# Cross attention's maxima ahead of a block's low split, its sums inside the second query projection, squares added on VectorE, and more halved products

## The chip, the cores and the metric

The kernel runs on one core of a Trainium2 chip. The metric is the device time of one execution in microseconds (us). The median of three runs of the kernel before is 655.46 us (655.09 to 655.58).

The names of the engines in the profile are: PE is TensorE (matmuls), PEld is the load of TensorE's stationary operand, DVE is VectorE, ACT is ScalarE, POOL is GpSimd, SP is SyncE, whose queue issues the loads of weights. PE, ACT, DVE and POOL each run their own queue in order and wait for each other by semaphores.

## The reference, cut to what matters

Two layers, 256 positions, width 1024, everything in f32. Each layer adds three parts to the hidden state `h`:

```
h = h + mixer(rmsnorm(h, norm_mix_g[layer]))
h = h + memory_cross_attention(rmsnorm(h, norm_xa_g[layer]), rmsnorm(mem, norm_mem_g[layer]), ...)
h = h + conv_ffn(rmsnorm(h, norm_ffn_g[layer]), ...)
```

- The mixer of layer 0 has 16 heads of width 64, eight of stick-breaking attention and eight of softmax attention with rotary queries and keys. That of layer 1 is 16 softmax heads with a forget gate. Both have a combined q/k/v projection (1024 x 3072) and an output projection (1024 x 1024).
- Cross attention has four heads of width 64: `q = h @ w_q` (1024 x 256), keys and values from `mem` (256 rows), a softmax over the 256 memory rows, and an output projection (256 x 1024).
- `conv_ffn` is a gated MLP: up (1024 x 5632), a causal depthwise convolution of width 3, silu times value, down (2816 x 1024).
- `rmsnorm(x, g) = x * rsqrt(mean(x*x) + 1e-6) * g`: it needs the sum of the squares of all 1024 channels of a row.

A last rmsnorm ends it.

## The kernel before, in words

**Layout and precision.** `h` is held transposed: eight tiles of 128 channels x 256 positions. A matrix product is done in three terms. Each operand is split into a high part (`fp32r`, an ACT copy) and a low part (DVE: the operand less its high part), and hi*hi, hi*lo and lo*hi are summed in PSUM; each is one PE instruction of 128x128 by 128x256. A projection onto 128 outputs over 1024 channels is thus 24 such products.

**Weights.** `block()` (L125) loads 128 x 1024 weights into `raw` through SP's queue, lets ACT write `whi` (L133) and DVE write `wlo` (L134), as a rule in two pieces of 512 columns, in the feed-forward part in one of 1024. Five pairs `whi`/`wlo` exist; a new block waits until PE has used the block five earlier.

**Order.** Only PE's order is written out by hand (L1046). The order of ACT, DVE and POOL is made by the framework's scheduler when the kernel is built, with the place of an instruction in the program as its priority. Two helpers bend it. `order()` puts one instruction behind another of the same engine. `fence(skip, on_act, on_dve)` (L122) makes the four blocks that follow after `skip` further blocks come behind the given instructions: their `whi` behind `on_act`, their `wlo` behind `on_dve`.

**Norms.** `rmsnorm`'s scale is applied late. `Normed.step()` writes the split of `h * g`: `xh` on ACT (L184), `xl` on DVE (L185). `Stats.add()` squares an `h` tile on ACT (L235) and adds it to the squares so far on POOL (L241). `Stats.sums()` (L261) sums over the partitions by four matmuls of one column (L266), DVE makes the mean (`ms`, L269) and POOL the power of -0.5 (`rcol`, L273). `spread()` (L277) turns that column into a row by two transposes on PE (L280) and an ACT copy. `residual()` (L566) adds a projection to `h[j]` on DVE (L567), then calls `Normed.step()` and `Stats.add()`.

**Mixer.** A `Pipe` counts projections with `tick()` and runs what is due at a count. `VISITS` says at which counts the attention of head pairs is done between projections (`visit()`, L611): outputs, scores, transposes or weights. In layer 0 `mem.spread` is due at count 16 by itself, between two projections (L632). At the end come eight blocks of the output projection: o0 to o3 (begun early), o4 to o6 in banks `sc`, o7 in a bank `acc`, each followed by its `residual`.

**Cross attention.** `cross()` (L797) projects q in two halves of 128 (channels 0 to 6 of both, then channel 7 of both), copies them out on DVE (`mq`, L806), and starts the value projection with a hook: after 13 of its 24 products come `st.sums()`, the score products of the four heads (L770), and the softmax: per head a maximum on DVE (`mx`, L778), a multiplication by `rcol` (L779), two exponentials on ACT (`xp`, L783), a reciprocal and two multiplications on DVE (L785, L787). Then come the second half of the value projection, transposes of the weights (L792), copies (`xpt`, L795), weights times values (L829), the split of the outputs (`gh`, `gl`), the output projection with its blocks `xa_o`, and eight residuals. The `fence` at L808 keeps the low splits of the `xa_o` blocks, and of the first two feed-forward blocks, behind the copy of the first `mq`.

**Feed-forward.** f counts 22 pairs of blocks. The pair f=0 is multiplied channel by channel, as `xh`, `xl` come in (L913). In f=1, `st.sums` is a hook after 6 products of the first block, `st.spread` one after 11 of the second.

**Halved products.** `product(..., halves)` (L286) does one product in two instructions of 128 columns with the same stationary operand. `HALVES` (L37) names the projections of the mixers in which one is halved, and the index of the product in it. In `proj_nat`, which makes v for positions 0 to 127 (t=0) and 128 to 255 (t=1), only t=0 can have one.

Of the kernel before, what the change touches and what calls it, by code (L numbers as in the profile page):

```python
# [17 lines left out]
P = 128  # L18
T = 256
# [16 lines left out]
           (26, (6, 7), (), ())))  # L36
HALVES = ({"q3": 8, "o3": 8}, {"k0": 18, "q1": 8, "k3": 8, "v2": 3, "q6": 8, "mk": 8, "o2": 8})  # L37
EPS = 1e-6
# [40 lines left out]
def trunk(ctx: ExitStack, tc: tile.TileContext, a: dict, out: bass.AP):  # L79
# [148 lines left out]
    class Stats:  # L228
# [4 lines left out]
        def add(self, t):  # L233
            sq = tmp.tile([P, T], F32, tag="sq", name="sq", bufs=3)
            nc.scalar.activation(sq, t, AF.Square)  # L235
            self.n += 1
            if self.n == KD and not self.one:
                self.parts = [self.acc, sq]
            else:
                if self.acc is not None:  # L240
                    nc.gpsimd.tensor_tensor(sq, sq, self.acc, op=ALU.add)  # L241
                self.acc = sq
                self.parts = [sq]
# [49 lines left out]

    def proj(b, off, xs, ps, first=True, last=True, m=P, hooks={}, skip=False, halve=None):
        n = 0
        for k, (xh, xl) in enumerate(xs):
            s = slice(off + k * m, off + k * m + m)
            end = last and k == len(xs) - 1
            for w, x in ((b.hi, xh), (b.hi, xl), (b.lo, xh)):
                product(ps[:m], w[:, s], x, n == halve, start=first and n == 0, stop=skip or end and w is b.lo,  # L300
                        skip_group_check=skip)
                n += 1
                if n in hooks:
                    hooks[n]()
        return ps
# [16 lines left out]

    def proj_nat(bs, xs, t, ps, hooks={}, halve=None):
        s = slice(t * P, (t + 1) * P)
        n = 0
        for k, (xh, xl) in enumerate(xs):
            b = bs[k // 4]
            w = slice((k % 4) * T, (k % 4 + 1) * T)
            for x, y in ((xh, b.hi), (xh, b.lo), (xl, b.hi)):
                product(ps, x[:, s], y[:, w], n == halve, start=n == 0, stop=n == 3 * KD - 1)  # L330
                n += 1
                if n in hooks:
                    hooks[n]()
# [258 lines left out]
    def mixer(layer, st, xs):  # L592
# [3 lines left out]
        pipe = Pipe()  # L596
        halves = HALVES[layer].get
        outs = [None] * 8
# [12 lines left out]
        def visit(out, prod, weigh):  # L611
# [12 lines left out]
            if layer == 0 and pipe.now == 8:  # L624
                rope_tables(st)
            for n in prod:
                for hd in heads[n]:
                    hd.scores()

        if layer == 0:  # L630
            pipe.at(13, mem.sums)
            pipe.at(16, lambda: mem.spread(bank(psO, "po")))  # L632
            pipe.at(6, lambda: rope_sines(heads[1][1].last))
# [3 lines left out]
        for g in range(4):  # L637
# [78 lines left out]
            def values():  # L716
                b = [block(w[6 * g + 2]), block(w[6 * g + 3])]
                for t in range(2):
                    ps = proj_nat(b, xs, t, (accA if g else accS)(),
                                  halve=None if t else halves(f"v{g}"))  # L720
                    v.append(evac_col(ps, st, t, "v", 6))
# [29 lines left out]
        for i in range(j, KD):  # L751
            residual(i, proj(block(w_out[i]), 0, outs, (accS, accS, accS, accA)[i - j]()), nst, nxt)
        return nst, nxt.res, ms, ks

    def mem_keys(layer, ms, pipe):
        ks = []
        for i in range(2):
            ps = proj(block(a["xa_k"][layer, i]), 0, ms, accA(), halve=None if i else HALVES[layer].get("mk"))
            ks.append(evac_row(ps, mem, "mk", False))
# [3 lines left out]
    class Cross:  # L763
# [10 lines left out]
        def scores(self):  # L774
            s = self.s
            mx = tiny.tile([P, 2], F32, tag="mx", name="mx", bufs=6)
            sm = tiny.tile([P, 2], F32, tag="sm", name="sm", bufs=6)
            nc.vector.tensor_reduce(mx, s.rearrange("p (t m) -> p t m", t=2), AX.X, ALU.max, negate=True)  # L778
            nc.vector.tensor_mul(mx, mx, self.st.col)  # L779
# [6 lines left out]
            for t, c in enumerate(cut):  # L786
                nc.vector.tensor_scalar(p[:, c], p[:, c], sm[:, t:t + 1], None, op0=ALU.mult)  # L787

        def weigh(self, copy):
# [7 lines left out]
    def cross(layer, st, xs, ms, ks):  # L797

        hd = []
        bq = [block(a["xa_q"][layer, i]) for i in range(2)]  # L800
        acc = [proj(bq[i], 0, xs[:7], accS(), last=False) for i in range(2)]
        for i in range(2):
            proj(bq[i], 7 * P, xs[7:], acc[i], first=False)
        for i in range(2):
            q = parts.tile([P, T], F32, tag="part", name="mq", bufs=NP)
            evac = nc.vector.tensor_scalar(q, acc[i], SCALE, None, op0=ALU.mult)  # L806
            if i == 0:
                fence(2, None, evac)  # L808
            hd += [Cross(j, q, ks[i], st) for j in range(2)]

        def scores():
            st.sums()
            both_products(hd[:2])
            both_products(hd[2:])
            for x in hd:
                x.scores()

        b = [block(a["xa_v"][layer, i]) for i in range(2)]
        v = [evac_col(proj_nat(b, ms, 0, bank(psO, "po", T), hooks={13: scores}), mem, 0, "mv", 2)]
        v.append(evac_col(proj_nat(b, ms, 1, accA()), mem, 1, "mv", 2))  # L820
        copied = [x.weigh(nc.vector.tensor_copy if i % 2 else nc.scalar.copy) for i, x in enumerate(hd)]
# [35 lines left out]
    def ffn(layer, st, xs):  # L857
# [58 lines left out]
        for f in range(KF):  # L916
# [3 lines left out]
            for i in range(2):  # L920
# [11 lines left out]
                else:  # L932
                    acc = (accS, accA)[i if full else n % 7 % 2]()
                    n += 1
                pss.append(proj(w, 0, xs if f < RAW else xn, acc, first=not (pair and i), hooks=hooks,
                                skip=pair, halve=20 if f == 1 and i == 1 else None))
            if f == 0:
# [201 lines left out]
```

## Time and profile before

| what | us |
|---|---|
| median of three runs (lowest, highest) | 655.46 (655.09, 655.58) |
| the profiled execution, its own time | 655.54 |
| its span, first to last instruction | 653.8 |
| PE busy in the span | 643.8 |
| DVE busy | 531.1 |
| ACT busy | 434.2 |
| POOL busy | 69.1 |
| mixer's last projections to the first feed-forward blocks, layer 0 | about 110 to 153 of the span |
| the same in layer 1 | about 430 to 473 of the span |

A busy time is the union of an engine's instructions. PE's instructions overlap, each lasts some 0.28 us and the next starts 0.113 us later, so PE's pace is read from starts or from counts, not from durations. In the chain (the instructions that ended last, followed back) each piece has its start, its share of the chain in us, and what it was. In the timeline a row has its start, its length with the count of merged instructions, and in brackets the idle time before it.

### The profile page before, as it was taken

The numbers are of one execution on the slowest core, as the hardware profiler recorded it, in microseconds if no ns is written. First come the engines' busy times: TensorE is split into PE (matmuls) and PEld (weight loads), VectorE is DVE, ScalarE is ACT, GpSimd is POOL, SyncE is SP. The second block draws the span as 40 slices with busy tenths as digits, with TensorE's granted clock in tenths as the row PEclk, the third lists the DMA queues.
The fourth block names the chain that finished last, engine by engine and source line by source line (L and its number), as shares of the span: only waits on it lengthen the run. The fifth ranks groups of instructions, "written<-read, shape, count | busy, mean of one in ns | idle before, by whom it ended". The sixth has DMA issues, their size and how long they took to land.

```text
span 653.8 us, 14583 instructions
## 1 busy us (share of the span) xinstructions
PE 643.8 (98%) x5632; PEld 628.9 (96%) x5632; DVE 531.1 (81%) x1099; ACT 434.2 (66%) x864; POOL 69.1 (11%) x84
## 2 busy tenths in 40 slices
PE   8999999999999999999999999999999999999996
PEld 6999999989999999999999999999899999999996
DVE  5879985999999999856578877778999999896442
ACT  6698865777787777554465676666878767784332
POOL 0001000216100000011114220021350000000000
PEclk9999999999999999999999999999999999999999
DMA  8967651645465766666648754326166578586501
GB/s 298 399 237 231 210 196 33 195 160 192 156 203 195 220 206 183 185 193 206 203 155 305 211 179 147 129 69 223 65 239 187 192 204 216 170 341 194 194 2 65
DMA packets 47814, 124.02 MB, mean 190 GB/s; under 512 B 13665, under 2 KB 17665, under 8 KB 47745
## 3 DMA queue, kind: packets, MB, share of 16 engines
q1 hardware_dynamic: 47456, 122.80, 57.6%
q8 instruction: 44, 0.72, 0.4%
q10 hardware_dynamic: 288, 0.30, 0.1%
q14 instruction: 26, 0.20, 0.1%
HBM read 119.90 MB, written 1.07 MB: 185 GB/s over the span
## 4 chain that ended last, share of the span: by engine, by line
PE 78%; DVE 10%; ACT 6%; DMA 2%; issue 2%; SPq 0%; POOL 0%; POOLq 0%; DVEq 0%; ACTq 0%
PE acc L292 41%; PE sc L292 23%; DVE wlo L134 5%; PE acc L981 3%; PE sc L981 3%; PE po L981 2%; DVE xl L185 2%; ACT whi L133 2%; PE po L439 2%; PE sc L404 1%; DMA raw<-xt 1%; PE sc L424 1%; DVE h L567 1%; PE po L292 1%; DMA raw<-ab_first 1%
## 5 line engine op out<-in xcount | busy, mean ns | idle before, releaser
L134 DVE TENSOR_TENSOR wlo<-raw,whi 128x512 fp32r<-128x512 f32 (+2 forms) x283 | 264.6, 957 | 55.1 <-ACT whi L133 53.4
L133 ACT ACTIVATE whi<-raw 128x512 fp32r<-128x512 f32 (+2 forms) x283 | 225.1, 828 | 91.1 <-PE acc L292 41.0
L292 PE MATMUL sc<-xn,whi 128*128 128x256 f32 x656 | 112.9, 276 | 0.0
L292 PEld LDWEIGHTS sc<-xn,whi 128*128 128x128 f32 x656 | 98.6, 188 | 0.0
L292 PE MATMUL sc<-xn,wlo 128*128 128x256 f32 x328 | 90.5, 276 | 0.0
L292 PE MATMUL acc<-xh,whi 128*128 128x256 f32 x287 | 80.7, 281 | 0.0
L292 PE MATMUL acc<-xn,whi 128*128 128x256 f32 x464 | 80.3, 276 | 0.0
L292 PE MATMUL acc<-xl,whi 128*128 128x256 f32 x288 | 79.8, 277 | 0.0
L292 PE MATMUL acc<-xh,wlo 128*128 128x256 f32 x282 | 78.3, 278 | 0.0
L292 PEld LDWEIGHTS acc<-xn,whi 128*128 128x128 f32 x464 | 69.8, 188 | 0.0
L292 PE MATMUL acc<-gh,whi 128*128 128x256 f32 x240 | 67.0, 280 | 0.0
L292 PE MATMUL acc<-gl,whi 128*128 128x256 f32 x240 | 66.2, 277 | 0.0
L292 PE MATMUL acc<-gh,wlo 128*128 128x256 f32 x236 | 65.2, 277 | 0.0
L292 PE MATMUL acc<-xn,wlo 128*128 128x256 f32 x232 | 64.0, 276 | 0.0
L292 PEld LDWEIGHTS sc<-xn,wlo 128*128 128x128 f32 x328 | 61.6, 188 | 0.0
L241 POOL TENSOR_TENSOR sq<-sq 128x256 f32<-128x256 f32 x35 | 29.0, 829 | 304.1 <-ACT sq L235 289.1
L292 PEld LDWEIGHTS acc<-xh,whi 128*128 128x128 f32 x287 | 54.0, 188 | 0.4
L292 PEld LDWEIGHTS acc<-xl,whi 128*128 128x128 f32 x288 | 54.2, 188 | 0.0
L292 PEld LDWEIGHTS acc<-xh,wlo 128*128 128x128 f32 x282 | 53.0, 188 | 0.0
L292 PEld LDWEIGHTS acc<-gh,whi 128*128 128x128 f32 x240 | 45.1, 188 | 1.1 <-ACT gh L180 0.8
L292 PEld LDWEIGHTS acc<-gl,whi 128*128 128x128 f32 x240 | 45.0, 188 | 0.0
L292 PEld LDWEIGHTS acc<-gh,wlo 128*128 128x128 f32 x236 | 44.3, 188 | 0.0
(283 smaller groups left out, 1534.4 us busy)
## 6 DMA issues: line engine op xcount, KB each, us to landing
raw<-up SPq DMA_DIRECT2D x88, 512.0 KB, 4.3
raw<-fox_in SPq DMA_DIRECT2D x24, 512.0 KB, 3.8
raw<-down_rows SPq DMA_DIRECT2D x22, 512.0 KB, 4.4
raw<-ab_in SPq DMA_DIRECT2D x20, 512.0 KB, 6.2
raw<-down SPq DMA_DIRECT2D x16, 448.0 KB, 3.3
raw<-ab_out SPq DMA_DIRECT2D x8, 512.0 KB, 3.7
raw<-down SPq DMA_DIRECT2D x8, 512.0 KB, 3.6
raw<-fox_out SPq DMA_DIRECT2D x8, 512.0 KB, 4.4
```

The lines of the kernel that those rows point to most:

```text
L133: i = nc.scalar.activation(hi[:, s], raw[:, s], AF.Copy)
L134: j = nc.vector.tensor_sub(lo[:, s], raw[:, s], hi[:, s].bitcast(F32))
L185: nc.vector.scalar_tensor_tensor(lo, src, g, hi.bitcast(F32), op0=ALU.mult, op1=ALU.subtract))
L241: nc.gpsimd.tensor_tensor(sq, sq, self.acc, op=ALU.add)
L292: nc.tensor.matmul(ps, st, mv, **kw)
L404: nc.tensor.matmul(s[:, c], q[:, qs], k[:, 0:n], start=i == 0, stop=True, skip_group_check=True)
L424: nc.tensor.transpose(self.s[:, c:c + P], self.p[:, c:c + P], ident)
L439: nc.tensor.matmul(po[i * DH:(i + 1) * DH, j * T + q:(j + 1) * T], v[m][:, vc + i * DH:vc + (i + 1) * DH], hd.pt[:, c], start=m == 0 and j ...
L567: nc.vector.tensor_add(h[j], ps, h[j])
L981: nc.tensor.matmul(ps[:, o:o + T], x[:, s], y[:, c + o:c + o + T], start=False, stop=k == KF - 1 and x is gl, skip_group_check=True)
```

## The change

Five edits are made.

1. `Stats.add()` adds the squares on VectorE instead of GpSimd.
2. In `cross()`, `st.sums()` is called after 9 products of the second query projection, and no longer behind 13 products of the value projection; the hook with the scores comes after 11 products of that instead of 13.
3. In `cross()`, the fence behind the first `mq` (`skip` 2, set ahead of the value blocks) is replaced by one behind the maximum of the fourth head (`skip` 0, set in the hook). Both bind the same four blocks: the two of `xa_o` and the first two of the feed-forward part.
4. In layer 0 `mem.spread` goes from count 16, where it stood alone, to count 17, behind that visit's transposes.
5. More products are halved. Both halves t of v can have one (an index of 24 or more means t=1).

```diff
-HALVES = ({"q3": 8, "o3": 8}, {"k0": 18, "q1": 8, "k3": 8, "v2": 3, "q6": 8, "mk": 8, "o2": 8})
+HALVES = ({"v1": 3, "q3": 8, "v2": 27, "v3": 27, "o3": 8, "o7": 2},
+          {"q0": 21, "k0": 18, "q1": 8, "v1": 3, "q3": 8, "k3": 8, "v2": 27, "q6": 8, "mk": 8, "o2": 8, "o7": 2})
...
-                    nc.gpsimd.tensor_tensor(sq, sq, self.acc, op=ALU.add)
+                    nc.vector.tensor_add(sq, sq, self.acc)
...
-                product(ps[:m], w[:, s], x, n == halve, start=first and n == 0, stop=skip or end and w is b.lo,
+                product(ps[:m], w[:, s], x, n in halve, start=first and n == 0, stop=skip or end and w is b.lo,
...
+        def halves(name, skip=0):
+            return (HALVES[layer].get(name, -1) - skip,)
...
+            if layer == 0 and pipe.now == 17:
+                mem.spread(bank(psO, "po"))
...
-            pipe.at(16, lambda: mem.spread(bank(psO, "po")))
...
-                                  halve=None if t else halves(f"v{g}"))
+                                  halve=halves(f"v{g}", 24 * t))
...
-            residual(i, proj(block(w_out[i]), 0, outs, (accS, accS, accS, accA)[i - j]()), nst, nxt)
+            residual(i, proj(block(w_out[i]), 0, outs, (accS, accS, accS, accA)[i - j](), halve=halves(f"o{i}")),
+                     nst, nxt)
...
-            nc.vector.tensor_reduce(mx, s.rearrange("p (t m) -> p t m", t=2), AX.X, ALU.max, negate=True)
+            found = nc.vector.tensor_reduce(mx, s.rearrange("p (t m) -> p t m", t=2), AX.X, ALU.max, negate=True)
...
+            return found
...
-        acc = [proj(bq[i], 0, xs[:7], accS(), last=False) for i in range(2)]
+        acc = [proj(bq[i], 0, xs[:7], accS(), last=False, hooks={9: st.sums} if i else {}, halve=(11,) if i else (2,))
+               for i in range(2)]
...
-            evac = nc.vector.tensor_scalar(q, acc[i], SCALE, None, op0=ALU.mult)
-            if i == 0:
-                fence(2, None, evac)
+            nc.vector.tensor_scalar(q, acc[i], SCALE, None, op0=ALU.mult)
...
-            st.sums()
             both_products(hd[:2])
             both_products(hd[2:])
-            for x in hd:
-                x.scores()
+            found = [x.scores() for x in hd]
+            fence(0, None, found[-1])
...
-        v = [evac_col(proj_nat(b, ms, 0, bank(psO, "po", T), hooks={13: scores}), mem, 0, "mv", 2)]
-        v.append(evac_col(proj_nat(b, ms, 1, accA()), mem, 1, "mv", 2))
+        v = [evac_col(proj_nat(b, ms, 0, bank(psO, "po", T), hooks={11: scores}, halve=(13,)), mem, 0, "mv", 2)]
+        v.append(evac_col(proj_nat(b, ms, 1, accA(), halve=(3,)), mem, 1, "mv", 2))
...
-                                skip=pair, halve=20 if f == 1 and i == 1 else None))
+                                skip=pair, halve=(8, 20)[i:i + 1] if f == 1 else ()))
```

More of the change, by code (lines that the diff above doesn't have):

```diff
@@ L292, in product, with proj @@
             nc.tensor.matmul(ps, st, mv, **kw)
-    def proj(b, off, xs, ps, first=True, last=True, m=P, hooks={}, skip=False, halve=None):
+    def proj(b, off, xs, ps, first=True, last=True, m=P, hooks={}, skip=False, halve=()):
         n = 0
@@ L320, in gates, with proj_nat @@
         return ps
-    def proj_nat(bs, xs, t, ps, hooks={}, halve=None):
+    def proj_nat(bs, xs, t, ps, hooks={}, halve=()):
         s = slice(t * P, (t + 1) * P)
@@ L329, in proj_nat @@
             for x, y in ((xh, b.hi), (xh, b.lo), (xl, b.hi)):
-                product(ps, x[:, s], y[:, w], n == halve, start=n == 0, stop=n == 3 * KD - 1)
+                product(ps, x[:, s], y[:, w], n in halve, start=n == 0, stop=n == 3 * KD - 1)
                 n += 1
@@ L596, in mixer @@
         pipe = Pipe()
-        halves = HALVES[layer].get
+        def halves(name, skip=0):
+            return (HALVES[layer].get(name, -1) - skip,)
         outs = [None] * 8
@@ L757, in mem_keys @@
         for i in range(2):
-            ps = proj(block(a["xa_k"][layer, i]), 0, ms, accA(), halve=None if i else HALVES[layer].get("mk"))
+            ps = proj(block(a["xa_k"][layer, i]), 0, ms, accA(), halve=() if i else (HALVES[layer].get("mk"),))
             ks.append(evac_row(ps, mem, "mk", False))
```

## The prediction, before the changed kernel was run

> **What bounds the kernel now.** I read the page's part 1, the windows of layer 0's passage from mixer to feed-forward, the chain, and then the timeline of single engines. First the page, its part 1 and one group of part 5:
>
> ```profile
> PE 643.8 (98%) x5632; PEld 628.9 (96%) x5632; DVE 531.1 (81%) x1099; ACT 434.2 (66%) x864; POOL 69.1 (11%) x84
> L241 POOL TENSOR_TENSOR sq<-sq 128x256 f32<-128x256 f32 x35 | 29.0, 829 | 304.1 <-ACT sq L235 289.1
> ```
>
> PE is busy for 98%, so what the change can save is a slower pace of PE here and there, and the few places where PE stands. The 35 additions on POOL are seven for each of five norms. In the windows, one per stage, the first number after the stretch is its length, and each engine's busy time follows:
>
> ```profile
> 110.50:117.40 6.90, 6.76 (x60) 6.56 (x58) 6.80 (x13) 6.20 (x15) 2.90 (x3) 1.00 0.09 14
> 117.40:125.70 8.30, 8.27 (x70) 8.27 (x71) 7.72 (x14) 5.32 (x13) 2.35 (x3) 1.00 0.74 246
> ...
> 143.60:149.80 6.20, 6.20 (x57) 6.20 (x56) 6.20 (x16) 5.39 (x15) 3.75 (x5) 1.00 0.45 143
> 149.80:153.00 3.20, 3.07 (x28) 2.88 (x26) 2.77 (x4) 3.20 (x5) 1.83 (x3) 1.00 0.00 0
> sum 42.50, PE 41.77 PEld 39.65 DVE 39.51 ACT 32.96 POOL 12.64; mean PE 5.97 PEld 5.66 DVE 5.64 ACT 4.71 POOL 1.81
> ```
>
> The order of columns is PE, PEld, DVE, ACT, POOL. In seven stretches that make up 42.50 us PE lacks 0.73 us, DVE 3.0. DVE is full at 110.5 to 117.4 and from 143.6 to 149.8. That is the bound of these passages, and PE's loss of 0.73 us a layer is what mending it can win, some 1.5 us in both (row by row a little more: a wait also empties PE's pipeline). In the chain of this stretch one sees where DVE holds PE:
>
> ```profile
> 113.13 1.22 DVE xl L185 x2
> 114.35 1.21 DVE wlo L134
> 115.56 0.89 DVE xl L185
> 116.45 0.34 DVE h L567
> 116.78 0.61 DVE wlo L134
> ...
> 117.43 2.86 PE sc L292 x22
> 120.29 2.83 PE acc L292 x24
> ...
> 144.70 0.40 DVE xl L185
> ...
> 146.17 1.48 DVE xl L185 x2
> 147.65 0.34 DVE h L567
> 147.98 0.55 DVE xl L185
> ...
> 149.42 0.34 DVE h L567
> ...
> 150.51 1.05 ACT whi L133
> ...
> 151.59 1.29 DVE wlo L134
> ...
> 152.92 0.74 PE sc L292 x4
> ```
>
> At 117.43 PE waits for the low part of o6, at 152.92 for that of the first block of f=1. The latter chain runs from the last `h` (from 149.42) over `xh`, `sq` and `whi` on ACT to `wlo`: 152.92 - 149.76 = 3.16 us behind the end of the last `h`. So the end of the eighth residual sets when the feed-forward part runs at PE's pace. From there on nothing but PE is in the chain until layer 1.
>
> **The change part by part.** *Squares on DVE.* An `xl` takes 0.40 us by the row at 144.70, a `wlo` piece 0.61 by that at 116.78. Beside POOL's additions they are longer: 1.22 for two `xl`, 1.21 for a `wlo`, 0.89, 1.48 for two, 0.55. POOL's rows:
>
> ```profile
> 113.11 3.06 POOL L241 TENSOR_TENSOR sq<-sq 128x256 f32<-128x256 f32 x3 [52.24 <-ACT sq L235]
> 145.74 6.04 POOL L241 TENSOR_TENSOR sq<-sq 128x256 f32<-128x256 f32 x7 [13.73 <-ACT sq L235]
> ```
>
> `h` stays at 0.34 in the same stretch; one of its inputs is in PSUM. An addition on DVE with both inputs in SBUF isn't timed by itself in these rows; between 0.34 (`h`) and 0.40 (`xl`), I take 0.34.
> Ahead of o6's low part the three additions cost DVE (1.22 - 0.80) + (1.21 - 0.61) + (0.89 - 0.40) = 1.5 us and will cost 3 x 0.34 = 1.0: PE's third product of o6 starts at 117.43, 0.34 us behind its place in the pace, and most of that goes: -0.3. This is then PE's gain up to the cross attention, and it only lasts if DVE is no later at the next two places.
> In the residuals of the cross attention the additions cost, until the last `h`, 0.68 (two `xl`) + 0.15 + 0.15 = 1.0 us. On DVE five of seven will stand ahead of it (program order: addition j follows `xl` j), 1.7 us: +0.7. Behind it, `wlo` of f=1 no longer meets POOL: 1.29 to 1.15 us, -0.14. In layer 0's down projection, where DVE has room, the same edit costs nothing.
> By the Trainium skill (Perfetto Trace Analysis, Optimizing Scalar/DVE Operations) VectorE and GpSimd share a read port of SBUF, so moving operations between them might not help. The trace agrees for the mixer's end (1.5 against 1.0) and puts it on the losing side at the cross attention's (1.0 against 1.7).
>
> *Sums and maxima.* The rows of what stands before the softmax:
>
> ```profile
> 128.83 0.74 DVE L806 TENSOR_SCALAR mq<-sc 128x256 f32<-128x256 f32 x2
> 129.50 1.28 DVE L134 TENSOR_TENSOR wlo<-raw,whi 128x512 fp32r<-128x512 f32 x2
> 130.77 1.28 DVE L134 TENSOR_TENSOR wlo<-raw,whi 128x512 fp32r<-128x512 f32 x2
> 131.97 1.28 DVE L778 TENSOR_REDUCE mx<-sc 128x2 f32<-128x512 f32 x2
> 140.57 1.22 DVE L134 TENSOR_TENSOR wlo<-raw,whi 128x1024 fp32r<-128x1024 f32 x1 [0.59 <-ACT whi L133]
> 130.14 0.50 PE L266 MATMUL acc<-const,sq 128*128 128x1 f32 x4
> 130.57 0.70 PE L770 MATMUL sc<-mk,mq 64*128 64x256 f32 x4
> 132.50 0.38 PE L292 MATMUL po<-wlo,gh 128*128 128x256 f32 x1
> ```
>
> The scores of the first two heads are ready at about 131.7 (half of the 1.9 us from 130.57 to 132.50, and PE's drain); DVE is with the fourth piece of `xa_o` until 132.0. So the fence alone gives the first maximum 0.3 us. Scores go off two products earlier (0.23), without the sums before them (0.43, the way from 130.14 to 130.57, paid instead inside the q projection), and with o6's 0.3: some 0.4 to 0.5 us earlier, 130.1. I count with maxima from 131.3, 0.65 earlier. The price is that DVE has nothing to do from `mq` (to 129.6 by its row, 129.2 with PE's gain) to 131.3, and four pieces of 0.6 us, 2.4 us, come later. About two fit into the gaps of 0.27 us between exponentials and into the 0.59 us before 140.57, and two delay the feed-forward `wlo` behind them. I put the first residual at 143.3 against 143.7: -0.35, bounds -0.7 (PE itself isn't ready sooner) and 0 (no piece finds a gap).
> With +0.7 - 0.35 - 0.14 the start of f=1 comes **0.2 us later per layer**, and whatever PE gained before is waited away there. Bounds: -0.7 (PE waits no more) to +0.95 (rival D). Moved `sums` also put `ms` ahead of the value blocks' `wlo` on DVE, 0.13 us as before, and `rcol` on POOL before it is needed; no SP issue moves.
>
> *Halved products and mem.spread.* PE has two paces, as the chain shows over the whole span, in rows of 24 products and of 72:
>
> ```profile
> 81.91 2.84 PE acc L292 x24
> ...
> 162.08 2.72 PE acc L292 x24
> ...
> 353.52 8.68 PE acc L292 x72
> ...
> 372.06 8.38 PE acc L292 x72
> ```
>
> That is 118 ns a product (2.84 / 24; 8.68 / 72 with the visit's drain) against 113 (2.72 / 24). Which pace comes after a visit looks like chance, and it stays until PE is disturbed. Behind every halved product of the trace the pace is the fast one. Its price is in these rows:
>
> ```profile
> 364.27 0.33 PE L290 MATMUL acc<-xh,wlo 128*128 128x128 f32 x2
> 364.44 0.33 PE L292 MATMUL acc<-xh,whi 128*128 128x256 f32 x1
> 364.61 0.28 PE L292 MATMUL acc<-xl,whi 128*128 128x256 f32 x1
> ```
>
> From 364.27 to 364.61 pass 0.34 us in place of 0.23, and a few products at 118 follow: 0.12 to 0.13 in all. At 4.6 ns (0.11 / 24) one pays from 27 products at 118 ns on. Where PE sets the pace: layer 1's v1 stands at the head of the 72 products at 118 ns, -0.30 + 0.13 = -0.17; layer 0's v1, at the head of 48 products, saves up to 0.08 if they go at 118 ns, -0.08; with `mem.spread` no longer alone, the 24 of the row at 81.91 that follow it need not go at 118 ns, -0.11. Those with some 20 products to the next visit (layer 0's v2 and v3, layer 1's q0, and v2, whose mark moves from t=0 to t=1) lose 0.03 to 0.05 each; layer 1's q3 comes when the pace is already restored, +0.12; the one in f=1 is even. Sum -0.1, bounds -0.5 (113 ns everywhere) and +0.4 (nothing to mend). Those in o7, q and v of the cross attention, five a layer, cost about 0.6 us, and would give back as much if all of the some 140 products from o6 to the transposes go at 118 ns, as those of the row at 120.29 are (2.83 us for 24); either way the wait at f=1 covers them, and they count in full if that wait goes.
> By the Trainium skill (TensorE: Matmul & The Clock Gate, Back-to-back issue gap) pairs of load and product at 128 columns sustain about 81 ns, so a halving would cost 162 - 113 = some 50 ns, an estimate from that page. The rows here say 120; the sum goes by them.
>
> **Sum.** 2 x 0.2 - 0.1 = +0.3 on the profiled execution's 655.54 us, of which 653.8 is the span. That execution is 0.08 above the median of the runs shown, so 655.54 + 0.3 - 0.08 = **655.8 us**, which can't be told from no change: a measurement here tells about 0.2%, 1.3 us.
>
> **The rivals.**
> *A. As summed*, 655.8: chance 0.37.
> *B. The additions find gaps.* If DVE's order puts them behind later `h` (three rather than five before the last), the start of f=1 is 0.4 earlier per layer: 655.5 - 0.8 - 0.1 = 654.6. For: the page's order of `h` and `xl` runs up to two ahead. Against: 143.6 to 149.8 has no gap. Chance 0.22, still no change.
> *C. PE alone bounds both passages.* All of PE's waits go, 0.7 per layer: 655.5 - 1.4 - 0.1 = 654.0. For: DVE's 1.5 and 1.7 us of collision go in full, and DVE lacked 3 us of being full over the passage. Against: the additions come back as 2.4 us. By the Trainium skill (SBUF — State Buffer, Who interferes with whom) a DVE instruction with two SBUF inputs and a GpSimd one that reads SBUF exclude each other for a whole instruction, which would free up to 0.8 us for each addition, more than it costs; the rows show 0.2 to 0.6. Chance 0.22, with the upper part of B.
> *D. Slower: additions pile up ahead of the eighth `h`.* Place: DVE, 143 to 150 and 463 to 470. If the scheduler takes `xl` 6 and addition 6 before `h` 7, that is 0.34 + 0.40 more, +0.95 per layer at f=1, as ACT's 1.7 us and `wlo` follow the `h`. With that 655.5 + 1.9 - 0.1 = 657.3. It decides from the point where an `h` waits for more than about 0.5 us behind additions. For: DVE is full there, and a full engine takes program order. Chance 0.17.
> *E. It doesn't do what it says*: the fence only idles DVE, or halvings fall where the pace is 113 ns anyhow: +0.4 to +1, 656.2. Chance 0.02.
>
> **How the numbers follow.** Faster by over 0.2% (below 654.15) is C with the edge of B: 0.25. Slower (above 656.8) is D with the edges of A and E: 0.20. Within: 0.55. The range goes from C's bound with all waits gone and good halvings, 653.8, to D with little gained, 657.4.
>
> **What would show it.** In the changed profile: no group on POOL for `sq`, 35 additions on DVE of some 0.4 us; `xl` at 0.40 throughout; no wait for o6's low part; the first maximum about 0.65 us earlier than 131.97, against PE's clock, and DVE idle before it; the first product of f=1's low part 3.0 us behind the last `h`, and at 153.1 if A is right, 152.5 with B, 152.2 with C, 153.9 with D; PE at 113 ns behind layer 1's v1 (8.3 us for what is 8.68 at 353.52). The forecast is wrong if PE stands at new places (for the last addition within q, say, or for `xa_o`'s low part), or if the slow pace spreads into the feed-forward part: 100 products at it are 0.46 us.

## The result, and the profile after

| | us | ratio to before (95% interval) |
|---|---|---|
| before, median (lowest to highest) | 655.48 (655.09 to 655.58) | |
| changed, median | 661.09 (660.99 to 662.10) | 1.009 (1.0073 to 1.0108) |
| changed, profiled execution: own time, span | 660.99, 659.2 | |

The change makes the kernel 5.6 us slower; the forecast was 655.8 and the range ended at 657.4. Line numbers of the changed kernel are one higher from L38 on, and more behind the added lines. Its page, part 1, and two groups of DVE in the view by line (columns as in the page's part 5):

```profile
PE 646.9 (98%) x5650; PEld 630.0 (96%) x5650; DVE 531.3 (81%) x1134; ACT 432.8 (66%) x864; POOL 40.8 (6%) x49
```
```profile
L186 DVE SCALAR_TENSOR_TENSOR xl<-h,small,xh 128x256 fp32r<-128x256 f32 x48 | 22.8, 479 | 6.4 <-ACT xh L185 6.3
...
L242 DVE TENSOR_TENSOR sq<-sq 128x256 f32<-128x256 f32 x35 | 14.6, 418 | 0.0
```

The same view of the kernel before, for `xl`:

```profile
L185 DVE SCALAR_TENSOR_TENSOR xl<-h,small,xh 128x256 fp32r<-128x256 f32 x48 | 31.8, 670 | 5.4 <-ACT xh L184 5.2
```

The edit does what it says: 35 additions have moved from POOL to DVE, an `xl` takes 479 ns in place of 670, and DVE's busy time is the same (531.3 against 531.1). So a sum of busy times does not show the loss. A ledger by stage does. Each stretch runs between two marks of the trace, as a rule the start of the first instruction of its kind; the spans are 653.76 and 659.20:

| stretch, us | layer 0 before | after | layer 1 before | after |
|---|---|---|---|---|
| last outputs of the mixer's heads to first cross scores | 24.42 | 24.47 | 26.50 | 26.55 |
| to the first maximum | 1.40 | 1.16 | 1.40 | 1.17 |
| to the end of the softmax's last multiplication | 6.78 | 7.44 | 7.05 | 7.71 |
| to the first weights times values | 0.44 | 0.44 | 0.44 | 0.44 |
| to the first residual | 4.44 | 5.04 | 4.44 | 5.04 |
| to the end of the eighth residual | 6.13 | 7.54 | 6.13 | 7.53 |
| to the sums in f=1 | 3.75 | 3.69 | 3.73 | 3.69 |

That is +2.42 and +2.44 us. Between layer 1's first product for its gates and its last head outputs there are another 0.51 (93.47 to 93.98), and all other stretches together change by 0.06. The loss thus has three places: the **eight residuals** (+1.41 a layer), the **softmax and what follows it** (-0.24 + 0.66 + 0.60 = +1.02 a layer), and **layer 1's mixer** (+0.51).

The residuals first. DVE's timeline in the changed kernel, layer 0 (start, length, engine and line, tiles, count, and in brackets the idle time before):

```profile
149.99 0.42 DVE L242 TENSOR_TENSOR sq<-sq 128x256 f32<-128x256 f32 x1
150.32 0.48 DVE L186 SCALAR_TENSOR_TENSOR xl<-h,small,xh 128x256 fp32r<-128x256 f32 x1
150.72 0.42 DVE L242 TENSOR_TENSOR sq<-sq 128x256 f32<-128x256 f32 x1
151.05 0.48 DVE L186 SCALAR_TENSOR_TENSOR xl<-h,small,xh 128x256 fp32r<-128x256 f32 x1
151.45 0.42 DVE L242 TENSOR_TENSOR sq<-sq 128x256 f32<-128x256 f32 x1
151.79 0.42 DVE L568 TENSOR_TENSOR h<-sc,h 128x256 f32<-128x256 f32 x1
```

Six of the seven additions and the seventh `xl` stand ahead of the eighth `h`, which is the last row (three additions are shown, three more came from 146.79 to 148.59). In the kernel before, the seventh `xl` stood behind the eighth `h`:

```profile
149.34 0.41 DVE L567 TENSOR_TENSOR h<-sc,h 128x256 f32<-128x256 f32 x1
149.68 1.51 DVE L185 SCALAR_TENSOR_TENSOR xl<-h,small,xh 128x256 fp32r<-128x256 f32 x2
```

ACT's timeline in the changed kernel shows who is left without work meanwhile:

```profile
149.04 0.51 ACT L185 ACTIVATE xh<-h,small 128x256 fp32r<-128x256 f32 x1 [0.98 <-DVE h L568]
...
152.24 0.51 ACT L185 ACTIVATE xh<-h,small 128x256 fp32r<-128x256 f32 x1 [0.96 <-DVE h L568]
...
152.96 3.89 ACT L134 ACTIVATE whi<-raw 128x1024 fp32r<-128x1024 f32 x4
```

ACT stands twice for an `h`, for 0.98 and 0.96 us, and all of f=1's `whi` and `wlo` wait behind its last split. In the chain of the changed kernel PE resumes at 155.31, where it did at 152.92. The chain shows the same order at the mixer's end, too:

```profile
114.87 0.42 DVE sq L242
115.29 0.34 DVE h L568
115.63 0.61 DVE wlo L135
...
116.28 1.76 PE sc L293 x13
...
154.03 1.24 DVE wlo L135
...
155.31 0.74 PE sc L293 x4
```

The second low piece of o5 now stands behind the additions and an `h`; PE waits for it at 116.28, 12 products ahead of the place where it waited in the kernel before (o6, 117.43), and for longer: the start there is 0.73 us after the one ahead of it, against 0.45 at 117.43 in the kernel before.

Then the softmax, DVE's timeline in the changed kernel:

```profile
129.10 0.77 DVE L813 TENSOR_SCALAR mq<-sc 128x256 f32<-128x256 f32 x2 [0.89 <-PE sc L293]
131.75 1.29 DVE L783 TENSOR_REDUCE mx<-sc 128x2 f32<-128x512 f32 x2 [1.88 <-PE sc L775]
...
135.61 0.67 DVE L135 TENSOR_TENSOR wlo<-raw,whi 128x512 fp32r<-128x512 f32 x1
136.19 0.61 DVE L792 TENSOR_SCALAR xp<-xp,sm 128x256 f32<-128x256 f32 x2
...
136.80 0.67 DVE L135 TENSOR_TENSOR wlo<-raw,whi 128x512 fp32r<-128x512 f32 x1
...
137.99 0.67 DVE L135 TENSOR_TENSOR wlo<-raw,whi 128x512 fp32r<-128x512 f32 x1
...
139.10 0.69 DVE L135 TENSOR_TENSOR wlo<-raw,whi 128x512 fp32r<-128x512 f32 x1
139.70 1.28 DVE L801 COPY xpt<-sc 128x512 f32<-128x512 f32 x2
```

DVE idles 0.89 + 1.88 us ahead of the first maximum, which comes 0.22 us earlier than at 131.97. Then the four freed pieces of `xa_o` run between a reciprocal and the multiplications that need it (three times), and ahead of the copies of the weights (once). In the kernel before they ran ahead of the first maximum, which they held up by some 0.2 us; now they are in the path.

### The profile page after: what moved, and what is told of

Read it like the earlier page. It is cut to its first block, busy times and chain, and to the rows that moved or that the text cites. A ratio compares the mean times of both kernels' runs of the same rounds, so it can differ in the third digit from the quotient of the medians.

```text
span 659.2 us, 14596 instructions
## 1 busy us (share of the span) xinstructions
PE 646.9 (98%) x5650; PEld 630.0 (96%) x5650; DVE 531.3 (81%) x1134; ACT 432.8 (66%) x864; POOL 40.8 (6%) x49
## 4 chain that ended last, share of the span: by engine, by line
PE 86%; DVE 7%; ACT 3%; issue 2%; DMA 1%; SPq 0%; POOLq 0%; POOL 0%; DVEq 0%; ACTq 0%
PE acc L293 44%; PE sc L293 24%; PE acc L985 3%; PE sc L985 3%; DVE wlo L135 2%; PE po L985 2%; PE po L440 2%; PE sc L677 1%; PE sc L405 1%; PE po L293 1%; PE sc L425 1%; ACT whi L134 1%; DVE sq L242 1%; DVE h L568 1%; DMA raw<-ab_first 1%
## 5 line engine op out<-in xcount | busy, mean ns | idle before, releaser
L293 PEld LDWEIGHTS acc<-xn,wlo 128*128 128x128 f32 x232 | 43.5, 188 | 0.0
```

Of the source, the lines that this page charges most:

```text
L293: nc.tensor.matmul(ps, st, mv, **kw)
```

## Experiments: the change taken apart

Each run compares a kernel with the kernel before on the same chip. Their medians and ratios (one of the five executions of the changed kernel with its additions on POOL took 1674.41 us, for a reason that the record doesn't show; the other four took 658.32 to 658.72):

| kernel | median us | before us | ratio (95% interval) |
|---|---|---|---|
| additions on DVE alone | 658.02 | 655.83 | 1.0036 (1.0023 to 1.0049) |
| sums, scores and fence alone | 657.81 | 655.83 | 1.0030 (1.0019 to 1.0040) |
| changed, additions on POOL | 658.63 | 655.83 | 1.0040 (1.0026 to 1.0054) |
| changed, old fence | 659.53 | 655.83 | 1.0054 (1.0039 to 1.0069) |
| halvings and `mem.spread` alone | 656.28 | 655.87 | 1.0007 (0.9998 to 1.0015) |
| sums and scores moved, old fence | 656.11 | 655.87 | 1.0004 (0.9995 to 1.0012) |
| additions on DVE, behind the eighth `h` | 656.33 | 655.87 | 1.0009 (1.0001 to 1.0018) |
| additions left out | 653.29 | 655.67 | 0.9960 (0.9947 to 0.9973) |
| halvings at other places | 655.77 | 655.67 | 1.0001 (0.9991 to 1.0010) |
| late additions, late hooks | 665.23 | 655.87 | 1.0160 (1.0136 to 1.0185) |
| late additions, early hooks | 659.93 | 655.67 | 1.0032 (1.0008 to 1.0056) |
| the same with earlier `mem.spread` | 660.03 | 655.67 | 1.0044 (1.0021 to 1.0066) |
| the same with two more halvings | 654.91 | 655.77 | 0.9986 (0.9977 to 0.9995) |
| before without f=1's halving | 661.89 | 655.77 | 1.0095 (1.0077 to 1.0114) |

**Additions on DVE alone.** One line of the kernel before:

```diff
-                    nc.gpsimd.tensor_tensor(sq, sq, self.acc, op=ALU.add)
+                    nc.vector.tensor_add(sq, sq, self.acc)
```


> The kernel before, with the additions of squares on VectorE and nothing else of the change. Theory one (the additions stand ahead of the last residual on DVE, about 1.3 us per layer at the end of the cross attention, and push o5's second low part behind them at the mixer's end, about 0.2 per layer): 658.3 to 658.8 us against 655.5, and the first low part of f=1 ends about 1.3 to 1.5 us later behind the first residual than before. Rival one (the price is only the difference of DVE time, 7 x 0.34 added less 1.7 us of collisions with POOL, in each layer): 656.8. Rival two (the fence and the halved products cost it all, the additions nothing): 655.5.

+2.19 us; first to eighth residual 7.55 us in both layers, against 6.13.

**The order in cross attention alone**: sums in the second query projection, scores after 11 products, fence behind the fourth maximum.

> The kernel before, with the sums inside the second query projection, the scores after 11 products and the fence behind the fourth maximum; additions on POOL, no new halved product, mem.spread where it was. Theory one (the four low splits of xa_o go between reciprocals and multiplications of the softmax and ahead of the copies of the weights: about 1 us per layer at the first residual): 657.3 to 657.8. Rival one (the splits fill DVE's gaps, and the earlier maxima win 0.4 to 0.7 per layer): 654.2 to 654.8. Rival two (the cost of the changed kernel is the additions alone): 655.5.

+1.98 us. The ledger shows 7.44 for the softmax and 5.04 to the first residual, as in the changed kernel, and 6.13 for the residuals, as before.

**The changed kernel less one of these**, the additions back on POOL, or the fence back behind the first `mq`:

> The changed kernel with the additions of squares back on GpSimd. Theory one (1.3 to 1.5 us per layer are the additions'): 658.0 to 658.5 against 661.1. Rival one (DVE is simply full, so that undoing either edit gives the same as undoing both): about 656. Rival three (the sums inside the q projection cost, since PE waits there for the last addition; POOL's is later than DVE's): slower than 661.

> The changed kernel with the fence of before (behind the first copy of q, two blocks later) in place of that behind the fourth maximum. Theory one (1 us per layer is the fence's): 658.8 to 659.3 against 661.1, and the first residual 1 us earlier behind the scores. Rival one (the fence only idles DVE for a time that DVE has): 661. Rival two (all of it is the additions, the fence helps): 661.5 or more.

658.63 and 659.53. The additions are worth 2.8 us within the change (5.61 - 2.80), the fence 1.9 (5.61 - 3.70), and the stretches in which the ledger shows each go back to their values of before (6.12 us for the residuals; 6.78 and 4.44 us for the softmax and what follows) without touching the other's. So these are two separate costs. Alone they came to 2.19 and 1.98 us.

**Halvings and `mem.spread` alone:**

> The kernel before with all the new halved products and the earlier mem.spread, and nothing else of the change: additions on POOL, sums and fence where they were. Theory one (a halving costs 0.12 us and in some places leaves the products behind it at the slow pace; the cover in layer 0 takes most of it, layer 1 pays about 0.5 us between the last heads and the gates): 0.3 to 0.9 us slower than before, 0.51 of it in layer 1's stretch from the last heads to the gates (93.98 against 93.47). Rival (each halving starts the fast pace, as the prediction had it): 0.1 to 0.4 us faster, that stretch at 93.4 or less.

+0.41 us, at the edge of what can be measured, and the stretch in layer 1's mixer is 93.98, exactly that of the changed kernel. The first theory's place and size hold; that every halving starts the fast pace is refuted. The three parts alone thus make 4.6 of the 5.6 us by the medians (2.19 + 1.98 + 0.41), and 5.3 of 5.4 by the spans of the profiled executions.

**Sums and scores moved, the fence left where it was:**

```diff
-        acc = [proj(bq[i], 0, xs[:7], accS(), last=False) for i in range(2)]
+        acc = [proj(bq[i], 0, xs[:7], accS(), last=False, hooks={9: st.sums} if i else {}) for i in range(2)]
```


> The kernel before with the sums inside the second query projection and the scores from 11 products on, the fence where it was (behind the first query copy). Theory one (all the cost of the reordering is the fence's, the sums are neutral): 655.5 to 656.2, with 1.6 us from scores to maxima, softmax stretch 6.78 and 4.44 from first weights product to first residual. Rival (moving the sums costs by itself): 656.5 to 657.5.

656.11, no difference that the interval can tell. The scores gain nothing: 24.39 us from the last head outputs to the first scores, against 24.42. Their wait to the maxima is 1.61, as DVE is still with the pieces of `xa_o`. So the cost of edits 2 and 3 is the fence's, as far as can be measured.

**Place, or time on DVE?** The same seven additions on DVE, kept back until the eighth `h` is done:

> The kernel before with the additions of squares on VectorE as in the change, but in cross attention all seven stand behind the eighth residual and its xl, ahead of the first low half of f=1. Same additions, same engine, another place. Theory one (it is their place ahead of the eighth residual that costs, since ScalarE's splits wait for it): the stretch from the first to the eighth residual 5.2 to 5.6 us against 7.54 when they stand between and 6.13 before; the stretch from the first residual to the sums in f=1 10.3 to 10.8 against 11.2, the run 656.2 to 657.2. Rival (VectorE's time alone counts, wherever the additions stand): first residual to the sums in f=1 11.1 to 11.3, the run 658.0 as with the additions between.

First to eighth residual 5.39 us in place of 7.55, first residual to the sums in f=1 10.42 in place of 11.24 (7.55 + 3.69); 656.33 against 658.02. DVE's timeline of this kernel:

```profile
148.54 0.42 DVE L587 TENSOR_TENSOR h<-sc,h 128x256 f32<-128x256 f32 x1
...
149.27 0.42 DVE L259 TENSOR_TENSOR sq<-sq 128x256 f32<-128x256 f32 x1
...
150.00 2.22 DVE L259 TENSOR_TENSOR sq<-sq 128x256 f32<-128x256 f32 x6
152.14 2.35 DVE L134 TENSOR_TENSOR wlo<-raw,whi 128x1024 fp32r<-128x1024 f32 x2
```

The eighth `h` starts 4.97 us behind the first (143.57), six additions then take 2.22 us in a row and delay f=1's low halves. Of the 1.36 us a layer that the additions cost when they stand between the residuals (11.24 - 9.88), their place accounts for 0.82, and their time on DVE, less the collisions that are gone, for 0.54. Both theories hold a part; the place is the larger one.

**The additions left out** on every engine, so that the sums of squares hold the last tiles alone: the floor.

> The kernel before with the additions of squares left out on every engine, so that the sums of squares hold the last tiles alone: the floor for what moving them can gain. Theory one (the gain to be had is the collisions of POOL with the residuals and what they push back): first to eighth residual 5.1 to 5.4 us against 6.13 in both layers, the run 653.6 to 654.6. Rival (the collisions are hidden, PE bounds these stretches): 655.0 to 655.8.

653.29, 2.4 us under before. First to eighth residual 5.40 in both layers, 0.73 less; the stretch before the first scores 0.95 and 0.99 less (23.47 and 25.51). So POOL's additions do cost the kernel before what the prediction saw in `xl` and `wlo`, and some 2.4 us is what moving them could win at most. The Trainium skill (Perfetto Trace Analysis, Optimizing Scalar/DVE Operations) warns that moving work between VectorE and GpSimd may not help as they share a read port. Here the collisions are real (0.73 us a layer at the residuals), and the move still made the residuals 1.41 us longer, by the experiment above more through its place in DVE's order than through its time.

How such a collision goes can be read in the kernel before, in the timelines of POOL and DVE around two of the additions:

```profile
117.77 0.81 POOL L241 TENSOR_TENSOR sq<-sq 128x256 f32<-128x256 f32 x1 [1.61 <-ACT sq L235]
120.79 0.80 POOL L241 TENSOR_TENSOR sq<-sq 128x256 f32<-128x256 f32 x1 [2.21 <-ACT sq L235]
```
```profile
117.91 0.96 DVE L185 SCALAR_TENSOR_TENSOR xl<-h,small,xh 128x256 fp32r<-128x256 f32 x1
120.92 0.96 DVE L185 SCALAR_TENSOR_TENSOR xl<-h,small,xh 128x256 fp32r<-128x256 f32 x1
```

Each `xl` starts shortly behind an addition and ends 0.29 us after it (118.87 against 118.58, 121.88 against 121.59). Of the 48 `xl` of this trace 25 start while an addition runs, and every one of them ends 0.28 to 0.29 us behind that addition's end, whether the `xl` started 0.13 us into it or 0.47. `h`, with one input in PSUM, stays at 0.41 to 0.42 us beside an addition. So an `xl` waits for the rest of the addition that it meets, and loses the more the earlier it comes.

## Experiments: PE's two paces

The new halvings did not do what the prediction took for granted. The chain of the changed kernel around layer 0's v3 and layer 1's k0 (start, share in us, count):

```profile
76.00 8.38 PE acc L293 x72
...
86.27 0.17 PE acc L291 x2
86.44 5.14 PE acc L293 x44
```
```profile
337.16 0.17 PE acc L291 x2
...
337.98 5.65 PE sc L293 x48
```

and of the kernel before at the same places:

```profile
76.04 5.65 PE acc L292 x48
...
86.06 5.56 PE acc L292 x48
```
```profile
335.52 5.44 PE sc L292 x48
```

With `mem.spread` out of the way, 72 products go at 116 ns with the start-up (8.38 / 72), where the last 24 had 118. But behind v3's halving the other 20 products of its group go at 118 ns all the same, and only the next group at 113 (5.14 us for the 44 together), as the next group did in the kernel before without any halving. Behind the halving of k0, which is there in both kernels, 48 products take 5.65 us after the change and 5.44 before. What differs next to it is that q0, just ahead, has a halving now. In the changed kernel's 31 halvings, 7 leave the products behind them at 118 ns; in the kernel before none of 13.

**The same halvings at other products of their groups:**

```diff
-HALVES = ({"v1": 3, "q3": 8, "v2": 27, "v3": 27, "o3": 8, "o7": 2},
-          {"q0": 21, "k0": 18, "q1": 8, "v1": 3,
+HALVES = ({"v1": 8, "q3": 8, "v2": 27, "v3": 32, "o3": 8, "o7": 2},
+          {"q0": 21, "k0": 8, "q1": 8, "v1": 8,
```


> The kernel before with the new halvings and mem.spread, where five of the halvings behind which the pace was not fast stand at another product of the same group: layer 0's v1 8 for 3 and v3 32 for 27, layer 1's k0 8 for 18 and v1 8 for 3, cross attention's v0 17 for 13 and v1 8 for 3. Theory (what decides is how the products around it lie in time, so that another place gives another outcome): most of the six run at 113 ns behind the new place, layer 1's stretch from the last heads to the gates near 93.7 against 93.98. Rival (these groups, in which weights are what moves, keep the slow pace wherever the halving stands): 118 ns behind at least four, the stretch at 93.9 to 94.1.

Four of the six run at 113 ns behind the new place. Two of these four, layer 0's v1 and cross attention's v1, tell nothing: with the halvings alone they were fast at the old place too (cross attention's v1 was slow there in the changed kernel). The other two are layer 1's v1 and k0, which were slow at the old place in both kernels; the 48 products behind k0 are back at 5.44 us:

```profile
336.49 5.44 PE sc L293 x48
```

Layer 1's stretch is 93.65, and the run can't be told from before. So of six moved halvings two changed the pace. A list of places that were good in one order isn't good in another: behind layer 0's v2, whose halving stands at the same product in three kernels, the pace is 113 ns in the changed kernel and in this one, and 118 with the halvings alone. What decides stays open.

**A version with the additions late.** In cross attention alone seven additions go to DVE, three behind the eighth `xl`, four behind the first low half of f=1; the sums and the spread come later:

```diff
+            if self.late:
+                sq = xin.tile([P, T], F32, tag="gh", name="sq", bufs=NG)
+                nc.scalar.activation(sq, t, AF.Square)
+                self.squares.append(sq)
+                if len(self.squares) == KD:
+                    self.gather(3)
+                return
...
-                hooks = ({6: st.sums}, {11: st.spread})[i] if f == 1 else {}
+                hooks = ({20: st.sums}, {24: st.spread})[i] if f == 1 else {}
...
+                    if i == 0:
+                        st.gather(4, w.made)
+                    else:
+                        order(w.made, st.gathered)
```


> A version made to beat the kernel before: in cross attention alone the seven additions go to VectorE, three behind the eighth xl and four behind the first low half of f=1, with the sums and the spread taken 14 and 13 products later in f=1; everything else as before. Theory one (what VectorE can do behind the last residual is free, and POOL's collisions with the residuals go): first to eighth residual 5.2 us against 6.13, 0.7 to 0.9 us less per layer, 653.9 to 654.6. Rival (PE waits for the sums or the spread instead, or the low halves of f=1 come late): 655.5 to 656.5.

The gain at the residuals came (5.39 us), and the run took 665.23. Both theories missed: most of the loss lies behind f=1. In the chain of this kernel:

```profile
158.71 0.17 PE acc L310 x2
...
159.28 0.22 PE acc L300 x2
159.50 2.83 PE sc L312 x24
```

The spread's two transposes (L300) came three products behind the halving (L310), and the feed-forward part went on at 118 ns (2.83 / 24). From the sums in f=1 on, layer 0 takes 5.9 us more up to the gates and layer 1 6.8 us more up to the end, although these stretches begin 14 products later; three starts that come 0.91 to 0.98 us after the one ahead of them (at 179.9, 506.6 and 518.9) are in that too. This is the profiled execution, of 670.96 us; the other five took 664.7 to 666.4, about one layer's loss less, and no trace shows how. The next kernel takes the sums at 12 and the spread at 11 of the second block, ahead of the halving at 20; another has `mem.spread` earlier as well.

> The late additions of the last run again, but the sums at 12 products of f=1's first block and the spread at 11 of its second, so that the spread stands ahead of the halved product at 20 as it did before. The last run's two layers lost 5.9 and 6.8 us behind f=1, where 1,500 products went at 118 ns and not at 113. Theory (a spread behind the halving leaves the slow pace to the whole of the feed-forward; the additions are not to blame): 113 ns behind f=1, the stretch from the sums of f=1 to the gates near 176.2, the run 654.6 to 655.2. Rival (the additions' place starves the feed-forward's splits): 118 ns or waits of PE remain, the run 657 or more.

> The same with mem.spread taken 0.8 us earlier in layer 0, as the change has it: the best version that I see. It removes the wait of 0.11 us at a gated key. Theory: 0.1 us under the late additions with early hooks, 654.5 to 655.1, the kernel before at 655.8. Rival (the 0.11 us turns up again at layer 0's next wait): the same time as without it.

In the profiled execution of the first everything came as expected: residuals 5.40, gates after 176.06 us, 113 ns behind f=1, 654.21. But its twelve executions lie in two groups, five at 654.21 to 654.92 and seven at 659.77 to 660.70; those of the second kernel four at 654.37 to 654.60 and eight at 660.00 to 660.89. So the expectation held for the smaller group only, the ratios in the table mix both groups, and 0.1 us from `mem.spread` can't be seen under that. The trace of the first shows one short wait in layer 0, at 191.3, ahead of the second product of f=8 (a start after 154 ns, and 113 again from the fifth product behind it on). Were the 1,218 products behind it at 118 ns, that would be 1,218 x 4.6 ns = 5.6 us, the distance of the groups. So the second kernel got two more halvings, of which the first is the very next product and the second stands in f=12:

```diff
-                                skip=pair, halve=20 if f == 1 and i == 1 else None))
+                                skip=pair, halve=20 if f == 1 and i == 1 else 2 if layer == 0 and f in (8, 12) and i == 0 else None))
```


> The late additions with early hooks and the earlier mem.spread, and two more halved products in layer 0's feed-forward, at f=8 and f=12, behind the place (f=7, 191.3 us) where the profiled execution shows one start 154 instead of 113 ns apart. That kernel's executions lay in two groups, 5 at 654.2 to 654.9 and 7 at 659.8 to 660.7; the 1,218 products behind that place would cost 5.6 us more at 118 than at 113 ns. Theory (in the second group this short wait ended the fast pace): nearly all executions at 654.4 to 655.4, at most 0.3 us for the halvings, faster than before by 0.6 to 1.2. Rival (the second group has another cause): a third or more of the executions stay at 659 or above.

All eleven executions lie between 654.50 and 655.87, the median is 654.91, ratio 0.9986 (0.9977 to 0.9995): the second group is gone, and this kernel is 0.9 us faster than the kernel before. The chain of its profiled execution, the slowest of the eleven:

```profile
189.07 3.02 PE sc L312 x26
192.09 0.17 PE sc L310 x2
...
194.78 2.83 PE acc L312 x24
...
214.81 0.17 PE acc L310 x2
214.98 2.45 PE acc L312 x21
217.43 2.72 PE sc L312 x24
```

A short wait comes just ahead of 192 (a start after 174 ns, at 191.81), and the halving follows with the next product. Behind both the pace is 118 ns (2.83 for 24); whether the wait or the halving brought it can't be told apart here. It lasts for some 190 products, up to the second halving at 214.81, and is 113 from there on (2.72). That makes 190 x 4.6 ns = 0.9 us, which is about what this execution lies above the median (655.87 against 654.91). That the 5.6 us of the second group come from the same place fits all this, but no trace of an execution of that group was kept, so it is not shown.

**One halving taken away** from the kernel before:

> The kernel before without the halved product at 20 of f=1, in both layers; the same arithmetic, one instruction less for each. Theory (a pace, once set, holds for the whole feed-forward): the 1,500 products behind it in layer 0 and the 960 in layer 1 start 118 ns apart instead of 113, the stretch from the sums of f=1 to the gates 183 to 184 against 176.7, the run 666 to 669. Rival (the pace comes back to 113 by itself, or does not depend on the halving): 655.4 to 656.

661.89 by two executions, +6.1. The windows of the kernel before, and then of this one, in stretches of 20 us in the feed-forward part of layer 0 and of layer 1 (length, PE's busy time and instructions, granted clock, DMA share, GB/s):

```profile
170.00:190.00 20.00, 20.00 (x179) 1.00 0.61 200
...
490.00:510.00 20.00, 20.00 (x178) 1.00 0.62 195
```
```profile
170.00:190.00 20.00, 20.00 (x179) 1.00 0.61 203
...
490.00:510.00 20.00, 20.00 (x172) 1.00 0.59 198
```

In layer 1 it is 172 products in 20 us instead of 178, at a granted clock of 1.00 and a busy share of 100% in both, and the stretch to the end is 186.92 us instead of 180.41. So in layer 1 the slow pace holds for the some 1,480 products up to the end. In layer 0 the fast pace came without the halving, so half the expectation missed. PE falls into one pace or the other and can keep it for very long, and in these traces a halving is one more throw.

## Why the prediction was wrong, step by step

- **Additions until the last `h`: +0.7 predicted, +1.41 measured.** The step that failed is "on DVE five of seven will stand ahead of it". Six do, and the seventh `xl` as well, which stood behind the eighth `h` before. It is rival D's order, for the reason given there, that a full engine takes program order, and D's price for this term too: 0.34 + 0.40 on top of the 0.7 make 1.44. DVE has no gap from the first `h` to the end of the eighth (busy for 7.53 of 7.53 us), so all of it comes out. That the price of one addition is 0.34 us was right (150.72 to 151.05, with the next start behind it). D's 0.95 for a whole layer was still too low against 2.4, as it kept the next term at -0.35.
- **First residual: -0.35 predicted, bounds -0.7 and 0; +1.02 measured.** "About two fit into the gaps of 0.27 us": a piece of 0.59 us does not fit into a gap of 0.27; it starts there and pushes the multiplications. Three pieces take 1.77 us, of which 0.66 come out as delay, and the fourth stands ahead of the copies in full, 0.60. The gaps were added up (three of 0.27 and one of 0.59) as if pieces could be cut to fit. The wrong sign was outside the stated bounds because "no piece finds a gap" was put at 0, while the pieces then cost up to 2.4.
- **Maxima 0.65 us earlier: 0.22 measured.** The scores start at 130.58, not at 130.1: o6's gain of 0.3 didn't come, and the longer wait at o5 took back the 0.23 of the two products.
- **o6's low part: -0.3 predicted.** The wait at o6 went, as foreseen, and came back at o5, a start after 0.73 us instead of 0.45. The prediction looked at one piece only; the additions stand ahead of the earlier piece as well. With the additions on DVE alone the stretch up to the scores is 0.21 us shorter in layer 0 (24.21) and 0.30 longer in layer 1 (26.80).
- **`wlo` of f=1, -0.14:** 0.06 measured (3.75 to 3.69).
- **Collisions with POOL:** right. `xl` is at its undisturbed length, and without additions the kernel is 2.4 us shorter. The prediction held the 0.2 to 0.6 us of its rows against rival C's exclusion for a whole instruction. The rows fit that exclusion: 0.2 to 0.6 us is what was left of the addition when the `xl` or `wlo` came. What C missed is that the additions came back in a worse place.
- **Halved products: -0.1 predicted, bounds -0.5 and +0.4; +0.51 in layer 1 and about 0 in layer 0.** `mem.spread` gained its 0.11, v3's halving lost as much. The largest single gain, -0.17 at layer 1's v1, didn't come: its 50 products behind the halving go at 117 to 118 ns as before, and the halving is paid on top. The price of a halving (0.12) was right; the sentence "behind every halved product of the trace the pace is the fast one" was true of 13 and is false of 7 among the changed kernel's 31. k0 was taken as unchanged, and lost 0.21.
- **The sum** had 2 x 0.2 - 0.1 = +0.3; the ledger gives 2 x 2.43 + 0.51 + 0.06 = +5.4. With the terms of the additions and of the first residual as measured it would have been 2 x (1.41 + 1.02 - 0.14) - 0.1 = +4.5. So these two are the failed steps, and the halvings the smaller rest.

## What to carry to other kernels

When work moves onto an engine that is already full, price its place in that engine's order and not only its duration: ask which instruction of the critical chain will stand behind it, and which engine then idles for that one. Deferred work is only free if an idle stretch as long as one whole piece lies behind the new place; pieces of 0.6 us in gaps of 0.27 us go into the path. And where PE runs on for thousands of products, look at the start-to-start time first: one halved product fewer ahead of such a stretch cost 6.1 us here, more than all five edits of the change together.

## What the runs showed of the hardware, unexpected

- PE's stream of 128x128 by 128x256 products keeps one of two paces, 113 or 118 ns from start to start, at the same granted clock (1.00) and with no wait in the profile, for up to 1,500 products. Where f=1's halving was taken away, the slow pace cost layer 1 6.5 us (186.92 against 180.41).
- The same program can run in two groups of times that lie 5.6 us apart (654.2 to 654.9 and 659.8 to 660.7, five and seven of twelve executions). The profiled executions show short waits of 40 to 60 ns; behind one the pace was 113 ns again within five products, behind another, with a halving right after it, 118. That such a wait makes the groups is likely and not shown.
- An `xl` on DVE, with both its large inputs in SBUF, that starts while an addition runs on POOL ends 0.28 to 0.29 us behind the addition's end, in all 25 cases of the kernel before. Over all 48 `xl` that is 670 ns on the mean against 479.
